# Projection products turned over: weight columns stationary, tokens moving, TensorE in program order

## The chip, the cores and the metric

The kernel runs on one core of one Trainium2 chip. The metric is the device time of one execution in microseconds (us). Five engines work side by side, each with a queue of its own that it takes in order: TensorE (PE in the profile; PEld is its weight load), VectorE (DVE), ScalarE (ACT), GpSimd (POOL) and SyncE (SP), which issues the transfers here.

## The reference

One layer of an encoder: 256 tokens, 2048 channels, all in float32. A bidirectional gated recurrence (16 heads of 128 keys and 128 values) and a gated feed-forward network with a width-3 convolution over tokens, each between RMS norms and with a residual.

```python
h = rmsnorm(x, norm_pre_mix)
u = h @ w_in                                   # 2048 -> [q | f_fwd | f_bwd | v | g], 2048 each
q = silu(q);  f = lb + (1 - lb) * sigmoid(f_raw);  k = 1 - f
# both directions: S_t = diag(f_t) S_{t-1} + k_t v_t^T,  o_t = S_t^T q_t
m = (rmsnorm(o, g_norm) * silu(g)) @ w_out
x = x + rmsnorm(m, norm_post_mix)
h = rmsnorm(x, norm_pre_ffn)
up = dwconv3(h @ ffn_w_in, w_conv)             # 2048 -> 11264, convolution over tokens
x = x + rmsnorm((silu(gate) * val) @ ffn_w_out, norm_post_ffn)
```

## The kernel before

Every dense product is cut into chunks of 512 output columns: 20 chunks of `w_in` (q, f, b, g, v for four groups of four heads), 4 of `w_o`, 22 of `w_up` and 4 of `w_dn`. A chunk runs over its input rows in parts of 256 rows (8 parts for 2048 rows, 22 in `w_dn`). For each part the weights come by DMA into `raw`; ScalarE rounds them to a high half `whi` (line 130), VectorE subtracts to get the low half `wlo` (line 131). `prep` does this up to `LOOK` = 3 parts ahead, in 4 buffers. The tokens are split the same way into `xh` and `xl`, and hi\*hi + hi\*lo + lo\*hi are added up in PSUM.

In `gemm` the tokens are stationary: for each 128 input rows and each of two token blocks, three products of 512 weight columns (lines 173, 176, 177). The result has tokens on the partitions. The recurrence and the convolution need channels on the partitions, so `two_tiles` (line 196) transposes q, f, b and the up-projection with eight 128x128 transposes a chunk.

The small work is cut into steps, which wait in two lists, `soon` and `later`; `gemm` takes one step after each part. `do_scores` queues the decayed scores of a group: `diag`, then seven levels of a binary tree over tokens (`level`), then `across`. A level is eight products of 128 columns (line 394), then VectorE work on keys `ks`, queries `qs`, block products `bp` and a masked copy into `Sd`, and a gather into `kc` on ScalarE. A level needs what the level ahead of it left. `do_o` multiplies scores with v, normalises and transposes back.

A scheduler orders the instructions of each engine. It keeps a few TensorE instructions in the order of the code (in the "head" and "tail" chunks); the others it may move. PSUM has 8 banks: `ps_g` (4) for the dense products, `ps_t` (2) for transposes, `ps_s` (2) for scores.

Of the kernel before, what the change touches and what calls it, by code (L numbers as in the profile page):

```python
# [13 lines left out]
U8 = mybir.dt.uint8  # L14
# [18 lines left out]
# the parts of the first projection, four heads at a time  # L33
# [3 lines left out]
# columns of the packed per-partition parameters  # L37
# [9 lines left out]
def encoder_layer(  # L47
# [34 lines left out]
    mk = const.tile([P, NLEV - 1, P], U8, name="mk")  # L82
# [51 lines left out]

    def flush():
        while soon or later:
            step()

    def gemm(xh, xl, order="plain", need=None, pre=None, mid=None):
# [16 lines left out]
        for s, m in seq:  # L156
# [13 lines left out]
            for j in range(2):  # L170
                k = 2 * s + j
                a, b = xh[:, k, m * P : (m + 1) * P], xl[:, k, m * P : (m + 1) * P]
                mm = nc.tensor.matmul(ps[m], a, hi[:, j, :], start=(k == 0), stop=False)  # L173
                if j == 0 and (order == "head" and s < 4 or order == "tail" and m == 1 and s >= nsub - 4):
                    tc.keep_in_program_order(mm)
                nc.tensor.matmul(ps[m], a, lo[:, j, :], start=False, stop=False)  # L176
                nc.tensor.matmul(ps[m], b, hi[:, j, :], start=False, stop=(k == 2 * nsub - 1))  # L177
# [5 lines left out]

    def rsqrt_mean(dst, ss, n):
        V.tensor_scalar(dst, ss, 1.0 / n, EPS, op0=ALU.mult, op1=ALU.add)
        G.tensor_tensor(dst, dst, mneg[:, : dst.shape[1]], op=ALU.pow)

    def two_tiles(dst_fn, srcs, after=None):
        """Four 128-column tiles of two token blocks, transposed, later on."""

        def one(i):
            tp = ps_t.tile([P, 2, T], F32, name="tp", tag="tp")
            for j in range(2):
                for m in range(2):
                    c0 = (2 * i + j) * P
                    nc.tensor.transpose(tp[:, j, m * P : (m + 1) * P], srcs[m][:, c0 : c0 + P], ident)  # L196
# [7 lines left out]
    xh = acts.tile([P, KT, T], F32R, name="xh", tag="ah")  # L204
    xl = acts.tile([P, KT, T], F32R, name="xl", tag="al")
# [4 lines left out]
    mkf = spool.tile([P, NLEV - 1, P], F32, name="mkf")  # L210
# [17 lines left out]
    def load_rest():  # L228
        nc.sync.dma_start(prm[:, C_CW:], par[:, C_CW:])
        nc.sync.dma_start(mkf, masks.rearrange("p (l t) -> p l t", t=P))  # L230
        V.tensor_copy(mk, mkf)

    # the tensor engine reaches its full clock after some microseconds of work
    warm = ps_t.tile([P, 2, T], F32, name="tp", tag="tp")
    for i in range(WARM):
        nc.tensor.transpose(warm[:, 0, :P], ident, ident)

    # lower bounds of the forget gates: softmax over the layers, cumulative
    # sum, minus the first layer's value
# [12 lines left out]
    def split_x(k2):  # L252
        tp = ps_t.tile([P, 2, T], F32, name="tp", tag="tp")
        for j in range(2):
            k = 2 * k2 + j
            for m in range(2):
                nc.tensor.transpose(tp[:, j, m * P : (m + 1) * P], xs[:, m, k * P : (k + 1) * P], ident)  # L257
        for j in range(2):
            k = 2 * k2 + j
            w1 = prm[:, C_PRE + k : C_PRE + k + 1]  # L260
            S.activation(xh[:, k, :], tp[:, j, :], AF.Copy, scale=w1)
        for j in range(2):
# [3 lines left out]
                xl[:, k, :], tp[:, j, :], w1, xh[:, k, :].bitcast(F32), op0=ALU.mult, op1=ALU.subtract  # L266
# [16 lines left out]
    nop = lambda: None  # L283
    split_x(0)
    split_x(1)
    ps0 = gemm(xh, xl, pre=lambda s: split_x(s + 2) if 2 * s + 4 < KT else None)
    soon.extend([lambda q=q: square_x(q) for q in range(4)] + [mean_x])
    ps1 = gemm(xh, xl)
# [3 lines left out]
    # ------------------------------------------------------- HGRN2, both ways  # L292
    opool = pool(hstack, "oacts", side="right")
    oh = opool.tile([P, KT, T], F32R, name="oh")
    ol = opool.tile([P, KT, T], F32R, name="ol")
# [11 lines left out]

    def do_q(g):
        ps = gemm(xh, xl) if g else ps0
        qn = [nat.tile([P, 512], F32, name="qn", tag="qn") for _ in range(2)]  # L310
        for m in range(2):
            silu_nat(ps, m, qn[m])
        qT = hp.tile([P, HG, T], F32, name="qT", tag="qT")
        two_tiles(lambda i, tp: S.copy(qT[:, 2 * i : 2 * i + 2, :], tp), qn)
        st["q", g] = qT

    def do_f(g, d):
        ps = gemm(xh, xl) if g or d else ps1
        sn = [nat.tile([P, 512], F32, name="qn", tag="qn") for _ in range(2)]
        for m in range(2):  # L320
            S.activation(sn[m], ps[m], AF.Sigmoid, scale=rs1[:, m : m + 1])
# [7 lines left out]
        def put(i, tp):  # L329
            for j in range(2):  # L330
                h = 2 * i + j
                c = d * NH + g * HG + h
                V.tensor_scalar(
                    f[:, h, :], tp[:, j, :], lb1[:, c : c + 1], lb[:, c : c + 1], op0=ALU.mult, op1=ALU.add
# [6 lines left out]
        two_tiles(put, sn, rest)  # L341
# [4 lines left out]
    def halves(t, m, c0=0, n=HG * T):  # L346
        """Of t[2, heads * tokens], the first of two in the left halves of blocks
        of 2m tokens and the second in the right halves: block, half, token."""
        return cut(t, c0, [[2 * m, n // (2 * m)], [HG * T + m, 2], [1, m]])

    def do_scores(g):
        """All decayed scores of four heads, S^T[s, t]: a pair (s, t) is met at
        the level of the binary tree over tokens where the two part, left and
        right in one block of 2m tokens, with the decay as a product up to the
        halves' boundary times one from there on. Forward, s lies left and t
        right; backward the other way round, so that both share a product.
        ks and qs hold the keys (forward, backward) and the queries (backward,
        forward) decayed to their block's boundary, bp the blocks' products."""
# [7 lines left out]
        def diag(i):  # L366
# [3 lines left out]
            sc = ps_s.tile([P, HG, P], F32, name="sc", tag="sc")  # L370
            for j in range(HG):
                h, b = (HG * i + j) // 2, (HG * i + j) % 2
                sl = slice(b * P, (b + 1) * P)
                nc.tensor.matmul(sc[:, j, :], kc[0][:, h, sl], q[:, h, sl], start=True, stop=True)  # L374
# [10 lines left out]
        def level(lev):  # L385
            m = 1 << lev
            scs = []
            for i in range(2):
                sc = ps_s.tile([P, HG, P], F32, name="sc", tag="sc")
                for j in range(HG):  # L390
# [3 lines left out]
                    nc.tensor.matmul(sc[:, j, :], kc[0][:, h, sl], r, start=True, stop=True)  # L394
# [20 lines left out]
        def across(d):  # L415
            sc = ps_s.tile([P, HG, P], F32, name="sc", tag="sc")
            s0, t0 = d * P, (1 - d) * P
            for h in range(HG):
                nc.tensor.matmul(  # L419
# [4 lines left out]
        later.extend([lambda: diag(0), lambda: diag(1)])  # L424
# [277 lines left out]
```

## Time and profile before

| what | value |
|---|---|
| median of 3 runs (lowest to highest) | 1385.48 us (1385.19 to 1386.78) |
| span of the profiled execution, first to last instruction | 1383.9 us |
| time of the profiled execution beside its span | not listed apart from the span |
| mean granted TensorE clock | 0.998 |
| TensorE busy; weight load busy | 1372.2 us; 1148.5 us |
| VectorE busy; ScalarE busy | 862.4 us; 684.1 us |

The profile is of one execution. Its span stands 1.6 us under the median of the runs. Durations of matmuls overlap: one of 512 columns is shown 0.39 us long while the next starts 0.23 us after it, so the spacing of starts, not the duration, is what one product costs TensorE.

### The profile page before, as it was taken

Reading aid. Unit: us, or ns where it says so; the run is one execution under the profiler, and the core shown is the slowest. Engines: PE = TensorE matmul, PEld = TensorE weight load, DVE = VectorE, ACT = ScalarE, POOL = GpSimd, SP = SyncE. Lnnn points to the kernel's source line nnn. Section 1 sums busy time; section 2 is a strip of 40 time slices with the busy share of each in tenths; the row PEclk is TensorE's granted clock in tenths of the full one; section 3 lists DMA queues with packets and bytes.
Section 4 is the critical chain, followed back from the end, with each engine's and each line's share of the span. In section 5 each row is a group of like instructions: output and inputs, shape, how many; then the busy total and the mean of one; then the engine's idle time right before and its main releaser. Section 6 shows DMA issues by size and latency. Waiting matters only on the chain.

```text
span 1383.9 us, 16448 instructions
## 1 busy us (share of the span) xinstructions
PE 1372.2 (99%) x6562; PEld 1148.5 (83%) x6562; DVE 862.4 (62%) x1007; ACT 684.1 (49%) x899; POOL 13.5 (1%) x21
## 2 busy tenths in 40 slices
PE   8999999999999999999999999999999999999997
PEld 7888888888888888888888888888888888888886
DVE  6577657855785776567566565656566656444444
ACT  6644544444444445456555555555555554434342
POOL 0000000000000000000000000000000000000000
PEclk9999999999999999999999999999999999999999
DMA  8553454445444534663555555555555556555552
GB/s 315 183 188 125 149 174 164 149 140 182 165 152 153 174 130 159 242 255 105 188 197 181 194 182 183 183 182 183 185 184 186 184 192 225 186 199 193 185 205 97
DMA packets 36988, 249.08 MB, mean 180 GB/s; under 512 B 4144, under 2 KB 4784, under 8 KB 7472
## 3 DMA queue, kind: packets, MB, share of 16 engines
q1 hardware_dynamic: 36912, 248.04, 51.9%
q8 instruction: 51, 0.84, 0.2%
q14 instruction: 25, 0.20, 0.0%
HBM read 245.93 MB, written 2.10 MB: 179 GB/s over the span
## 4 chain that ended last, share of the span: by engine, by line
PE 98%; DMA 1%; issue 0%; SPq 0%; DVE 0%; ACT 0%; DVEq 0%; POOLq 0%; POOL 0%
PE pg L176 30%; PE pg L177 30%; PE pg L173 30%; PE sc L394 4%; PE tp L196 2%; DMA xs<-in_x 1%; PE sc L451 1%; PE sc L419 1%; PE sc L374 1%; PE sc L450 1%; PE tp L545 0%; PE tp L257 0%; DVE fw L639 0%; SPq L116 0%; SPq L213 0%
## 5 line engine op out<-in xcount | busy, mean ns | idle before, releaser
L131 DVE TENSOR_TENSOR wlo<-raw,whi 128x1024 fp32r<-128x1024 f32 (+1 forms) x457 | 557.2, 1221 | 426.1 <-ACT whi L130 425.7
L130 ACT CAST whi<-raw 128x1024 fp32r<-128x1024 f32 (+1 forms) x457 | 479.6, 1051 | 506.8 <-PE pg L177 486.9
L177 PE MATMUL pg<-whi,h2l 128*128 128x512 f32 x704 | 276.3, 392 | 0.0
L176 PE MATMUL pg<-wlo,h2h 128*128 128x512 f32 x704 | 276.2, 392 | 0.0
L173 PE MATMUL pg<-whi,h2h 128*128 128x512 f32 x704 | 276.1, 393 | 0.0
L173 PE MATMUL pg<-whi,xh 128*128 128x512 f32 x640 | 251.6, 395 | 0.0
L177 PE MATMUL pg<-whi,xl 128*128 128x512 f32 x640 | 251.4, 393 | 0.0
L176 PE MATMUL pg<-wlo,xh 128*128 128x512 f32 x640 | 250.9, 392 | 0.0
L177 PEld LDWEIGHTS pg<-whi,h2l 128*128 128x128 f32 x704 | 132.3, 188 | 28.3
L176 PEld LDWEIGHTS pg<-wlo,h2h 128*128 128x128 f32 x704 | 132.3, 188 | 26.2
L173 PEld LDWEIGHTS pg<-whi,h2h 128*128 128x128 f32 x704 | 132.2, 188 | 25.9
L177 PEld LDWEIGHTS pg<-whi,xl 128*128 128x128 f32 x640 | 120.2, 188 | 24.6
L176 PEld LDWEIGHTS pg<-wlo,xh 128*128 128x128 f32 x640 | 120.3, 188 | 23.4 <-DVE wlo L131 0.2
L173 PEld LDWEIGHTS pg<-whi,xh 128*128 128x128 f32 x640 | 120.3, 188 | 23.3
L177 PE MATMUL pg<-whi,gl 128*128 128x512 f32 x352 | 137.0, 389 | 0.0
L173 PE MATMUL pg<-whi,gh 128*128 128x512 f32 x352 | 137.0, 389 | 0.0
L176 PE MATMUL pg<-wlo,gh 128*128 128x512 f32 x352 | 137.0, 389 | 0.0
L176 PEld LDWEIGHTS pg<-wlo,gh 128*128 128x128 f32 x352 | 66.1, 188 | 13.8
L173 PEld LDWEIGHTS pg<-whi,gh 128*128 128x128 f32 x352 | 66.1, 188 | 13.7
L177 PEld LDWEIGHTS pg<-whi,gl 128*128 128x128 f32 x352 | 66.1, 188 | 13.6
L394 PEld LDWEIGHTS sc<-qs,kc 128*128 128x128 f32 x448 | 57.9, 192 | 2.2
L607 DVE SCALAR_TENSOR_TENSOR acc<-tp,prm,acc 128x255 f32<-128x255 f32 x88 | 41.8, 476 | 27.3 <-PE tp L196 27.3
(108 smaller groups left out, 1010.6 us busy)
## 6 DMA issues: line engine op xcount, KB each, us to landing
raw<-in_w_up SPq DMA_DIRECT2D x88, 1024.0 KB, 4.9
raw<-in_w_in SPq DMA_DIRECT2D x78, 1024.0 KB, 4.9
raw<-in_w_dn SPq DMA_DIRECT2D x44, 1024.0 KB, 4.9
raw<-in_w_o SPq DMA_DIRECT2D x16, 1024.0 KB, 4.9
x<-in_x SPq DMA_DIRECT2D x1, 2048.0 KB, 7.6
wp<-in_post SPq DMA_DIRECT2D x2, 1024.0 KB, 5.9
out<-fw SPq DMA_DIRECT2D x8, 256.0 KB, 2.5
xs<-in_x SPq DMA_DIRECT2D x3, 512.0 KB, 10.2
```

The lines of the kernel that those rows point to most:

```text
L130: S.copy(hi[:, j], src[:, j])
L131: V.tensor_tensor(lo[:, j], src[:, j], hi[:, j].bitcast(F32), op=ALU.subtract)
L173: mm = nc.tensor.matmul(ps[m], a, hi[:, j, :], start=(k == 0), stop=False)
L176: nc.tensor.matmul(ps[m], a, lo[:, j, :], start=False, stop=False)
L177: nc.tensor.matmul(ps[m], b, hi[:, j, :], start=False, stop=(k == 2 * nsub - 1))
L196: nc.tensor.transpose(tp[:, j, m * P : (m + 1) * P], srcs[m][:, c0 : c0 + P], ident)
L374: nc.tensor.matmul(sc[:, j, :], kc[0][:, h, sl], q[:, h, sl], start=True, stop=True)
L394: nc.tensor.matmul(sc[:, j, :], kc[0][:, h, sl], r, start=True, stop=True)
L419: nc.tensor.matmul(sc[:, h, :], ks[:, d, h, s0 : s0 + P], qs[:, 1 - d, h, t0 : t0 + P], start=True, stop=True)
L450: nc.tensor.matmul(o[:, h, :], Sd[:, 2 * h + b, :], v[:, b, cs], start=True, stop=False)
L451: nc.tensor.matmul(o[:, h, :], So[1 - b][:, h, :], v[:, 1 - b, cs], start=False, stop=True)
L607: V.scalar_tensor_tensor(a[:, 1:T], z[:, 0 : T - 1], cw[0], a[:, 1:T], op0=ALU.mult, op1=ALU.add)
```

## The change

The chunks of q, f, b (12 chunks) and of `w_up` but the first (21 chunks) go through a new function, `gemm_t`. There the weight columns are stationary and the tokens move: `xh` and `xl` lie side by side in one tile `xx` of 2 x 256 columns, so that one product of 512 columns with `whi` gives hi\*hi in the left half of a PSUM bank and hi\*lo in the right half, and a second product of 256 columns adds `wlo` times `xh` to the left half. Channels come out on the partitions, and the transposes of these chunks go. `each_token` adds the halves (a copy on ScalarE, an add on VectorE per 128 channels) and multiplies by the norm's factor per token, which `spread` lays out over the partitions with two small products. A chunk takes 4 PSUM banks instead of 2, so `ps_g` has 6, and scores share `ps_t` with the transposes. All TensorE instructions go through `mm` and `tr`, which keep them in the order of the code. The lists get empty steps (`nop`): a level every second step, `do_o` behind the scores in `later`. The masks come as bytes by DMA, behind the start-up loads.

```diff
+    def mm(out, a, b, **kw):
+        return tc.keep_in_program_order(nc.tensor.matmul(out, a, b, **kw))
+    def tr(out, a):
+        return tc.keep_in_program_order(nc.tensor.transpose(out, a, ident))
-    ps_g = pool(ctx, "ps_g", 4, space=bass.MemoryType.PSUM)
+    ps_g = pool(ctx, "ps_g", 6, space=bass.MemoryType.PSUM)
     ps_t = pool(ctx, "ps_t", 2, space=bass.MemoryType.PSUM)
-    ps_s = pool(ctx, "ps_s", 2, space=bass.MemoryType.PSUM)
...
+    def gemm_t(xx, need=None, pre=None):
+        ps = [ps_g.tile([P, 2, T], F32, name="pg", tag="pg") for _ in range(4)]
+        for s in range(nsub):
+            if pre:
+                pre(s)
+            prep(base + s + (LOOK if ci else 1))
+            hi, lo = parts[ci, s]
+            for n in range(4):
+                cs = slice(n * P, (n + 1) * P)
+                for j in range(2):
+                    k = 2 * s + j
+                    mm(ps[n], hi[:, j, cs], xx[:, k], start=(k == 0), stop=False)
+                    last = k == 2 * nsub - 1
+                    mm(ps[n][:, 0, :], lo[:, j, cs], xx[:, k, 0, :], start=False, stop=last)
+            step()
...
+    def spread(rs, name):
+        tp = ps_t.tile([P, 2, T], F32, name="tp", tag="tp")
+        for m in range(2):
+            a = rs[:, m : m + 1].broadcast_to([P, P])
+            mm(tp[:, 0, m * P : (m + 1) * P], a, ident, start=True, stop=True)
+        S.copy(name, tp[:, 0, :])
...
+    def each_token(ps, dst, r):
+        for i, p in enumerate(ps):
+            z = dst[:, i, :]
+            S.copy(z, p[:, 1, :])
+            V.tensor_tensor(z, p[:, 0, :], z, op=ALU.add)
+        V.tensor_tensor(dst, dst, r[:, None, :].broadcast_to([P, len(ps), T]), op=ALU.mult)
...
     def do_q(g):
-        ps = gemm(xh, xl) if g else ps0
...
-        two_tiles(lambda i, tp: S.copy(qT[:, 2 * i : 2 * i + 2, :], tp), qn)
+        ps = gemm_t(xx) if g else ps0
+        each_token(ps, qT, r1)
+        S.activation(sg, qT, AF.Sigmoid)
+        V.tensor_tensor(qT, qT, sg, op=ALU.mult)
...
-        later.extend([lambda: diag(0), lambda: diag(1)])
-        later.extend([lambda lev=lev: level(lev) for lev in range(NLEV)])
-        later.extend([lambda: across(0), lambda: across(1)])
+        later.extend([nop, lambda: (diag(0), diag(1))])
+        for lev in range(NLEV):
+            later.extend([nop, lambda lev=lev: level(lev)])
+        later.extend([nop, lambda: (across(0), across(1))])
...
-        soon.extend([lambda: one(0), lambda: one(1)])
-        two_tiles(put, og)
+        queue = soon if g == NG - 2 else later
+        queue.extend([nop, lambda: one(0), lambda: one(1), nop])
+        two_tiles(put, og, queue)
...
     def up(c, done):
-        ps = gemm(h2h, h2l) if c else ps0
+        ps = gemm_t(hh) if c else ps0
...
+        z = [fn.tile([P, 2, T], F32, name="un", tag="un") for _ in range(2)]
+        for i in range(2):
+            each_token(ps[2 * i : 2 * i + 2], z[i], r2)
+        soon.extend([lambda: put(0, z[0]), lambda: put(1, z[1]), lambda: done(acc)])
```

Three places show how instructions move. The first is TensorE at the start, from the warm-up transposes (`tp<-ident`) on. Transposes `tp<-ident,xs` turn x; eight of them are one 512 KB piece of x. Before:

```order
L236 MATMUL tp<-ident 128x128 x18
L257 MATMUL tp<-ident,xs 128x128 x8
L173 MATMUL pg<-whi,xh 128x512
L176 MATMUL pg<-wlo,xh 128x512
L173 MATMUL pg<-whi,xh 128x512
L176 MATMUL pg<-wlo,xh 128x512
L177 MATMUL pg<-whi,xl 128x512
```

Now:

```order
L140 MATMUL tp<-ident 128x128 x18
L140 MATMUL tp<-ident,xs 128x128 x12
L137 MATMUL pg<-xx,whi 128x512
L137 MATMUL pg<-xx,wlo 128x256
L137 MATMUL pg<-xx,whi 128x512
L137 MATMUL pg<-xx,wlo 128x256
```

Four more transposes, which read the third piece of x, stand ahead of the first dense product; and the products come as pairs of 512 and 256 columns.

The second place is ScalarE around the end of the second chunk (f of group 0) and the start of the third (b). `qT` are the queries, `pg` the PSUM tiles of a chunk. Before:

```order
L130 CAST whi_449<-raw_447 128x1024
L303 ACT_TABLE_LOAD
L303 ACTIVATE sg_536<-pg_161,rs1_142 128x512
L303 ACTIVATE sg_539<-pg_162,rs1_142 128x512
L130 CAST whi_469<-raw_447 128x1024
```

Now (`pg_380` to `pg_383` are the four tiles of the f chunk):

```order
L224 COPY rt_79<-tp_562 128x256
L129 CAST whi_657<-raw_631 128x1024
L356 ACT_TABLE_LOAD
L356 ACTIVATE qn_610<-qT_600 128x1024
L347 COPY qn_613<-pg_380 128x256
L347 COPY qn_613<-pg_381 128x256
L347 COPY qn_613<-pg_382 128x256
L347 COPY qn_613<-pg_383 128x256
```

The table load stood in the middle of the second chunk and read two PSUM tiles of the first; now it and a sigmoid of 1024 columns stand ahead of the four copies that empty the f chunk's PSUM tiles.

The third place is VectorE between the b chunk of a group and its diagonal scores, which read `kc`. Before:

```order
L131 TENSOR_TENSOR wlo_778<-raw_775,whi_777 128x1024
L333 TENSOR_SCALAR f_559<-tp_743,lb1_132,lb_131 128x256 x2
L333 TENSOR_SCALAR f_559<-tp_766,lb1_132,lb_131 128x256 x2
L131 TENSOR_TENSOR wlo_802<-raw_775,whi_801 128x1024
L338 TENSOR_SCALAR ks_560<-f_559 128x1024
L339 TENSOR_TENSOR qs_561<-qT_542,f_559 128x1024
L405 TENSOR_TENSOR bp_857<-f_559 128x1024
L369 TENSOR_TENSOR kc_793<-ks_560 128x1024
```

Now:

```order
L130 TENSOR_TENSOR wlo_844<-raw_821,whi_843 128x1024
L348 TENSOR_TENSOR qn_805<-pg_630,qn_805 128x256
L349 TENSOR_TENSOR qn_805<-qn_805,rt_79 128x1024
L130 TENSOR_TENSOR wlo_864<-raw_861,whi_863 128x1024
L375 TENSOR_SCALAR f_624<-qn_805,lb1_127,lb_126 128x256 x4
L130 TENSOR_TENSOR wlo_880<-raw_861,whi_879 128x1024
L380 TENSOR_SCALAR ks_625<-f_624 128x1024
L381 TENSOR_TENSOR qs_626<-qT_600,f_624 128x1024
L447 TENSOR_TENSOR bp_959<-f_624 128x1024
L411 TENSOR_TENSOR kc_895<-ks_625 128x1024
```

The row of work up to `kc` stays, with the adds and the multiplication of `each_token` ahead of it; on TensorE the diagonal scores that wait for `kc` now stand at a fixed place, behind the fourth part of the chunk after b; the scheduler had put those of group 0 behind the sixth.

More of the change, by code (lines that the diff above doesn't have):

```diff
@@ L171, in gemm @@
                 k = 2 * s + j
[L172 to L177, printed above, removed]
+                a, b = (xx[:, k, i, m * P : (m + 1) * P] for i in range(2))
+                mm(ps[m], a, hi[:, j, :], start=(k == 0), stop=False)
+                mm(ps[m], a, lo[:, j, :], start=False, stop=False)
+                mm(ps[m], b, hi[:, j, :], start=False, stop=(k == 2 * nsub - 1))
             if m == 1 or order == "head" and s < 4:
@@ L182, in gemm @@
         return ps
+    def gemm_t(xx, need=None, pre=None):
+        ci = at["chunk"]
+        at["chunk"] += 1
+        nsub = 2 * chunks[ci][2]
+        base = subs.index((ci, 0))
+        ps = [ps_g.tile([P, 2, T], F32, name="pg", tag="pg") for _ in range(4)]
+        for s in range(nsub):
+            if s == need:
+                flush()
+            if pre:
[10 more added lines that the diff above has]
+            step()
+        return ps
     def rsqrt_mean(dst, ss, n):
@@ L195, in one @@
                     c0 = (2 * i + j) * P
-                    nc.tensor.transpose(tp[:, j, m * P : (m + 1) * P], srcs[m][:, c0 : c0 + P], ident)
+                    tr(tp[:, j, m * P : (m + 1) * P], srcs[m][:, c0 : c0 + P])
             dst_fn(i, tp)
@@ L199, in one @@
                 after()
-        soon.extend([lambda: one(0), lambda: one(1)])
-    xh = acts.tile([P, KT, T], F32R, name="xh", tag="ah")
-    xl = acts.tile([P, KT, T], F32R, name="xl", tag="al")
+        queue.extend([lambda: one(0), lambda: one(1)])
+    xx = acts.tile([P, KT, 2, T], F32R, name="xx", tag="xx")
     hstack = ExitStack()
@@ L229, in load_rest @@
         nc.sync.dma_start(prm[:, C_CW:], par[:, C_CW:])
-        nc.sync.dma_start(mkf, masks.rearrange("p (l t) -> p l t", t=P))
-        V.tensor_copy(mk, mkf)
     warm = ps_t.tile([P, 2, T], F32, name="tp", tag="tp")
     for i in range(WARM):
-        nc.tensor.transpose(warm[:, 0, :P], ident, ident)
+        tr(warm[:, 0, :P], ident)
     lbr = prm[:, C_LB : C_LB + 2 * NH].rearrange("p (n l) -> p n l", l=1)
@@ L256, in split_x @@
             for m in range(2):
-                nc.tensor.transpose(tp[:, j, m * P : (m + 1) * P], xs[:, m, k * P : (k + 1) * P], ident)
+                tr(tp[:, j, m * P : (m + 1) * P], xs[:, m, k * P : (k + 1) * P])
         for j in range(2):
@@ L293, in encoder_layer @@
     opool = pool(hstack, "oacts", side="right")
[L294 to L295 removed]
+    oo = opool.tile([P, KT, 2, T], F32R, name="oo")
+    mk = opool.tile([P, NLEV - 1, P], U8, name="mk")
+    nc.sync.dma_start(mk, masks.rearrange("p (l t) -> p l t", t=P))
     rstack = ExitStack()
@@ L544, in split @@
             for j in range(4):
-                nc.tensor.transpose(tp[:, j, :], x2[:, m, n * 512 + j * P : n * 512 + (j + 1) * P], ident)
+                tr(tp[:, j, :], x2[:, m, n * 512 + j * P : n * 512 + (j + 1) * P])
             for j in range(4):
@@ L578, in encoder_layer @@
     rsqrt_mean(rs2, sx2, D)
+    r2 = const.tile([P, T], F32, name="rt", tag="rt")
+    spread(rs2, r2)
     bstack.close()
```

110 lines of the change are left out of this document (54 added, 56 removed).

## The prediction

> **What bounds the kernel now.** I read the page's busy times and its chain of waits first, then the waits by engine, then stretches of one stage each.
>
> ```profile
> PE 1372.2 (99%) x6562; PEld 1148.5 (83%) x6562; DVE 862.4 (62%) x1007; ACT 684.1 (49%) x899; POOL 13.5 (1%) x21
> PE 98%; DMA 1%; issue 0%; SPq 0%; DVE 0%; ACT 0%; DVEq 0%; POOLq 0%; POOL 0%
> ...
> PE tp L257 <- DMA xs<-in_x: 2.4, 2, 1.8
> PE tp L236 <- POOL ident masks.py:199: 1.4, 1, 1.4
> ```
>
> TensorE is on the chain for 98% of the span, and in the whole run it waits twice for x (2.4 us) and once for the identity (1.4 us). It is a queue that never runs dry, so the time is the sum of the spacings of its products. Work taken from it counts in full; every wait that appears on it counts in full too. The spacings come from two stretches, `w_o` chunk 3 with nothing but 96 products of 512 columns, and twenty chunks of the up-projection:
>
> ```profile
> 589.06:610.82 21.76, 21.76 (x97) 18.02 (x96) 12.18 (x12) 11.49 (x14) 0.00 (x0) 1.00 0.54 192
> 658.13:1112.71 454.58, 454.58 (x2082) 375.23 (x2080) 283.20 (x340) 245.21 (x302) 0.35 (x1) 1.00 0.54 186
> ```
>
> The first gives 21.76 / 96 = 226.7 ns for a wide product (512 columns). The second gives 454.58 / 20 = 22.73 us a chunk; it has eight transposes beside the 96 products, so a transpose costs (22.73 - 21.76) / 8 = 0.121 us with the disturbance around it.
>
> **What is removed.** The twelve q, f, b chunks and 21 of the 22 up chunks lose eight transposes each: 264 x 0.121 = **-32.0 us**, all on the path. What ScalarE and VectorE did with them goes too, and is off the path.
>
> **What replaces it.** Per 128 rows and chunk, six wide products (1360 ns) become four pairs of a wide and a narrow one (256 columns). The moved columns are the same, 3072; the products go from 6 to 8. So everything hangs on the narrow one's spacing: each ns over 113.4 (half of 226.7) costs 33 x 64 = 2112 times that, 2.1 us. No row shows this shape. The nearest:
>
> ```profile
> 709.45 0.60 PE L196 MATMUL tp<-ident,un 128*128 128x128 f32 x4
> 363.15 1.95 PE L374 MATMUL sc<-qT,kc 128*128 128x128 f32 x16
> L374 PE MATMUL sc<-qT,kc 128*128 128x128 f32 x64 | 7.8, 275 | 0.0
> L374 PEld LDWEIGHTS sc<-qT,kc 128*128 128x128 f32 x64 | 7.8, 191 | 0.3
> L173 PEld LDWEIGHTS pg<-whi,h2h 128*128 128x128 f32 x704 | 132.2, 188 | 25.9
> ```
>
> A row of 16 score products is 1.95 us long, the last 0.275: spacing (1.95 - 0.275) / 15 = 111.7 ns, each with its own weight load. For transposes, (0.60 - 0.27) / 3 = 110 ns. The loads of scores are shown 191 ns long, those of dense products 188; since score products follow each other every 111.7 ns, a load of this kind does not hold TensorE for 188. So the low end is 109 (transposes, rounded down), the high end 226.7 (the width saves nothing). I take 115: half of the wide one, and 1.6 ns for a part that doesn't shrink; it lies by the rows of 110 and 112, the fastest at which weights are changed here. Then a pair is 341.7 against 340.0 ns: **+3.6 us** (-9 at 109, +14 at 120, +236 at 226.7). `spread` adds four small products, **+0.5**.
>
> [...]
>
> **What the fixed order costs.** Where the scheduler let TensorE go round a wait, it now stands. I followed the new order of each queue with durations of before; VectorE instructions that follow each other without waiting overlap by about 0.08 us.
>
> *Start.* The first dense product now stands behind the transposes of the third piece of x.
>
> ```profile
> 1.36 4.10 PE L236 MATMUL tp<-ident 128*128 128x128 f32 x18 [1.36 <-POOL ident masks.py:199]
> 7.93 0.63 PE L257 MATMUL tp<-ident,xs 128*128 128x128 f32 x4 [1.81 <-DMA xs<-in_x]
> 8.32 0.48 PE L173 MATMUL pg<-whi,xh 128*128 128x512 f32 x1
> ...
> 12.31 1.06 PE L257 MATMUL tp<-ident,xs 128*128 128x128 f32 x8 [0.55 <-DMA xs<-in_x]
> ```
>
> That piece lands at 12.3. Before, dense products began at 8.32; now at 12.31 + 4 x 0.11 = 12.75. The chunk then takes 21.9 us and 20 more transposes (2.4), ending at 37.0 instead of 33.76: **+3.3**. And TensorE idles from 8.4 to 12.3, with only four transposes since 6.1. What that does to the clock:
>
> ```profile
> 5.80:9.21 3.41, 1.60 (x11) 1.26 (x10) 2.03 (x4) 1.97 (x5) 0.00 (x0) 1.00 1.01 308
> 1374.55:1377.96 3.41, 1.39 (x7) 0.81 (x5) 1.52 (x4) 0.69 (x2) 0.54 (x1) 1.00 0.61 218
> 1377.96:1383.90 5.94, 0.00 (x0) 0.00 (x0) 2.34 (x4) 0.00 (x0) 0.00 (x0) 0.50 0.49 177
> ```
>
> The granted clock (third from the end) is 1.00 behind a stretch of 3.41 us with 1.60 of work, 0.50 behind one with 1.39. The warm-up row shows the low clock's price: (4.10 - 0.4) / 17 = 0.22 us a transpose, twice the 0.11. After 12.3 I expect half speed for about 3.2 us: **+1.6** (0.7 to 2.5).
>
> *First b chunk.* ScalarE loads a table, runs a sigmoid and only then empties the f chunk's PSUM tiles.
>
> ```profile
> L303 ACT ACT_TABLE_LOAD x1 | 1.3, 1283 | 0.0
> L130 ACT CAST whi<-raw 128x1024 fp32r<-128x1024 f32 x455 | 478.3, 1053 | 503.7 <-PE pg L177 486.9 <-DVE ks L338 8.5 <-DMA raw<-in_w_in 3.0
> L616 ACT ACTIVATE acc<-acc 128x1024 f32<-128x1024 f32 x11 | 11.6, 1057 | 0.0
> L602 ACT ACTIVATE acc<-tp,prm 128x256 f32<-128x256 f32 x88 | 37.1, 477 | 35.4 <-PE tp L196 35.4
> L339 DVE TENSOR_TENSOR qs<-qT,f 128x1024 f32<-128x1024 f32 x8 | 9.7, 1218 | 0.0
> ```
>
> From the f chunk's end: a cast whose buffer comes free then (1.05), the load (1.28), the sigmoid (1.06), while VectorE still has q's multiplication (1.22) ahead of its adds: first tile free at about 3.45 + 1.22 + 0.48 (an add of that size taken as long as the copy) = 5.15 us. Four of six banks are the f chunk's, so b's third tile needs it after two tiles of work, 1.37 us: **+3.8**. A gap that long takes the work of one or two stretches of 3.41 under 1.4 us: half speed again, **+1.0**. [...] In the other chunks the first tile is free about when the chunk ends, 1.4 us early.
>
> *Diagonal scores*, at their fixed place after four parts (10.9 us after the b chunk):
>
> ```profile
> 354.50 0.69 DVE L338 TENSOR_SCALAR ks<-f 128x1024 f32<-128x1024 f32 x1
> 355.11 1.22 DVE L339 TENSOR_TENSOR qs<-qT,f 128x1024 f32<-128x1024 f32 x1
> 356.24 1.22 DVE L405 TENSOR_TENSOR bp<-f 128x1024 f32<-128x1024 f32 x1
> 357.38 1.22 DVE L369 TENSOR_TENSOR kc<-ks 128x1024 f32<-128x1024 f32 x1
> ```
>
> These four take 4.1 us, ending 12.7 us after that b chunk (345.89). In the new order they follow the fourth `wlo` of the next chunk, which can't end before 7.8: `kc` at 11.9, four groups x 1.0 = **+4.0** (0 to 7).
>
> *Levels.* In two steps TensorE works 2 x 2.72 + 8 x 0.112 = 6.3 us; VectorE, by the rows below, two `wlo`, `ks`, `qs` and two masked copies, 2 x 1.22 + 1.21 + 1.22 + 2 x 0.74 less six overlaps = 5.9. I cost them at nothing; the cover is 0.4 us a level.
>
> ```profile
> L413 DVE COPY_PREDICATED Sd<-mk,sc 128x512 f32<-128x512 uint8 x48 | 35.3, 735 | 12.3 <-PE sc L394 12.2
> L398 DVE TENSOR_TENSOR ks<-ks,bp 128x1024 f32<-128x1024 f32 x24 | 29.0, 1209 | 0.0
> L131 DVE TENSOR_TENSOR wlo<-raw,whi 128x1024 fp32r<-128x1024 f32 x455 | 555.9, 1223 | 423.6 <-ACT whi L130 423.2
> ```
>
> *Ends.* The last group's transposes are flushed inside the first `w_o` chunk, and the norm factor goes through TensorE behind the first up chunk, where ScalarE waited for it:
>
> ```profile
> L186 POOL TENSOR_TENSOR ro<-ro,mneg 128x4 f32<-128x4 f32 x8 | 8.1, 1010 | 503.4 <-DVE ro L185 503.4
> L468 ACT ACTIVATE oh<-tp,prm 128x512 fp32r<-128x512 f32 x8 | 5.1, 685 | 6.2 <-PE tp L196 6.2
> 658.51 1.27 ACT L594 ACTIVATE un<-pg,rs 128x512 f32<-128x512 f32 x2 [1.85 <-POOL rs L186]
> ```
>
> Squares (1.0), factor (0.2 + 1.0) and four products (1.1) stand between the last scores and the flush, against one part of 2.7: 0.8 us, and 0.7 for the split (0.685): **+1.5**. The factor came 0.4 us after the chunk's end at 658.13: **+0.5**.
>
> *Queues.* SyncE's bytes of masks now wait for x's last reader with weights queued behind, some 5 us before those weights must be issued: nothing. GpSimd keeps its work. VectorE gains at most 33 x (4 x 0.48 + 1.22) = 104 us and ScalarE 33 x 4 x 0.48 = 63 from `each_token`: 70% and 54% busy.
>
> **Sum.** -32.0 + 3.6 + 0.5 + 3.3 + 1.6 + 3.8 + 1.0 + 4.0 + 1.5 + 0.5 = -12.2: a span of 1371.7, and with the 1.6 us by which the runs' median stands above this profile's span, **1373 us**.
>
> **Rivals.**
> - *No waits* (the fixed order costs nothing, so it and the wider steps do nothing): -32.0 + 4.1 = 1358. For it: before, TensorE never waited for VectorE. Against: x cannot land earlier. Chance 0.08.
> - *Narrow product at the floor*, 109: 1361 with my waits. For it: two rows of 110 to 112 with half the columns. Chance 0.12. [...]
> - *Waits at every chunk's edge*: `each_token` comes late by 0.3 us of its 1.4 us cover at 33 edges, +10: 1383 (1380 to 1390). For it: VectorE's 104 us more, all at the edges. Against: the order puts the adds first. Chance 0.20.
> - *Slower: the narrow product doesn't cover the weight load.* It decides from 115 + 12.2 / 2.112 = 120.8 ns; at the load's shown 188 it would be 1373 + 154 = 1527. Against: scores at 111.7 with loads of 191. Chance 0.08.
>
> The forecast itself (1366 to 1380) has 0.52. About 0.2% is what a measurement here can tell from no change: 1382.7 to 1388.3. Range 1360 to 1386: below lie parts of the first two rivals, above part of the third and the slower one. Faster 0.78 (forecast, two rivals, a third of the third), same 0.11, slower 0.11.
>
> **What would show it.** An up chunk of 21.9 us (22.73 now); the first product at 12.7; granted clock 0.5 behind it; one wait of some 4 us in the first b chunk for VectorE; four of 1 us for `kc`. Wrong, if up chunks take over 22.5 us, or waits for VectorE on TensorE pass 20 us in sum.

## The result: 12 us slower, and the profile after

The changed kernel took 1398.14 us (median of 4 runs, 1397.63 to 1399.16), the kernel before 1386.13 in the same comparison (1385.19 to 1386.83): ratio 1.0088, 95% interval 1.0074 to 1.0102. Forecast were 1373 us, 1360 to 1386. The profiled run spans 1396.8 us, 12.9 more than before. Its page and its chain of waits:

```profile
span 1396.8 us, 18404 instructions
...
PE 1373.8 (98%) x7362; PEld 1180.3 (84%) x7362; DVE 935.1 (67%) x1188; ACT 698.7 (50%) x971; POOL 12.4 (1%) x21
...
PE 96%; DVE 2%; ACT 1%; issue 1%; DMA 0%; SPq 0%; DVEq 0%; POOLq 0%; POOL 0%; ACTq 0%
```

TensorE still carries the end. What it waits for (us in total, times, longest):

```profile
PE sc L137 <- DVE kc L411: 4.1, 4, 1.0
PE pg L137 <- DVE qn L348: 3.7, 1, 3.7
PE tp L140 <- DVE wlo L130: 3.4, 1, 3.4
PE tp L140 <- DMA xs<-in_x: 1.4, 1, 1.4
PE tp L140 <- POOL ident masks.py:199: 1.4, 1, 1.4
PE pg L137 <- DVE oo L512: 0.6, 1, 0.6
PE tp L140 <- DVE og L504: 0.2, 1, 0.2
```

That is 14.8 us against 3.8 before, and the large ones had been forecast. What had not been is the pace of the products. `w_o` chunk 2 and nineteen up chunks (2 to 20), and the groups of the second stretch:

```profile
603.82:625.58 21.76, 21.76 (x98) 18.02 (x97) 11.91 (x11) 11.30 (x14) 0.00 (x0) 1.00 0.56 196
696.81:1126.46 429.65, 429.65 (x2434) 372.52 (x2433) 315.01 (x439) 235.00 (x323) 0.00 (x0) 1.00 0.54 186
...
L137 PE MATMUL pg<-hh,whi 128*128 128x512 f32 x1217 | 430.1, 399 | 0.0
L137 PE MATMUL pg<-hh,wlo 128*128 128x256 f32 x1217 | 341.8, 281 | 0.0
```

The old form in `w_o` is as it was, 21.76 us a chunk. An up chunk takes 429.65 / 19 = 22.61 us; 22.73 before, 21.9 forecast. It holds nothing but 64 pairs of a wide and a narrow product, so a pair costs 429.65 / 1216 = 353.3 ns, where 341.7 was forecast and 340 is what six wide products made of it before. Starts of products one by one:

```profile
799.27 0.40 PE L137 MATMUL pg<-hh,whi 128*128 128x512 f32 x1
799.51 0.28 PE L137 MATMUL pg<-hh,wlo 128*128 128x256 f32 x1
799.63 0.40 PE L137 MATMUL pg<-hh,whi 128*128 128x512 f32 x1
799.87 0.28 PE L137 MATMUL pg<-hh,wlo 128*128 128x256 f32 x1
799.98 0.40 PE L137 MATMUL pg<-hh,whi 128*128 128x512 f32 x1
800.22 0.28 PE L137 MATMUL pg<-hh,wlo 128*128 128x256 f32 x1
800.33 0.40 PE L137 MATMUL pg<-hh,whi 128*128 128x512 f32 x1
...
800.69 0.40 PE L137 MATMUL pg<-hh,whi 128*128 128x512 f32 x1
```

From wide to wide: 0.36, 0.35, 0.35, 0.36. In the trace's ns the pairs take 361, 349 and 350 in turn, with wide spacings of 241, 236 and 233 and narrow ones of 120, 113 and 117. So from the narrow product's start to the next one it takes about what was forecast, and the **wide one behind it became longer** than its 226.7. In the first projection some stretches between two groups of score products run in this rhythm of three, others at 346.7 a pair (343 and 350 in turn). Counting stretches of five pairs and more, 1724 pairs are in the first rhythm and 315 in the second, and none changes within a stretch.

### The profile page after: what moved, and what is told of

Same layout as the page of the kernel before. It is cut to its first block, busy times and chain, and to the rows that moved or that the text cites. A ratio compares the mean times of both kernels' runs of the same rounds, so it can differ in the third digit from the quotient of the medians.

```text
span 1396.8 us, 18404 instructions
## 1 busy us (share of the span) xinstructions
PE 1373.8 (98%) x7362; PEld 1180.3 (84%) x7362; DVE 935.1 (67%) x1188; ACT 698.7 (50%) x971; POOL 12.4 (1%) x21
## 4 chain that ended last, share of the span: by engine, by line
PE 96%; DVE 2%; ACT 1%; issue 1%; DMA 0%; SPq 0%; DVEq 0%; POOLq 0%; POOL 0%; ACTq 0%
PE pg L137 89%; PE sc L137 6%; PE tp L140 1%; ACT whi L129 1%; DVE wlo L130 1%; DMA raw<-in_w_in 0%; DVE bp L447 0%; DVE kc L411 0%; DVE ks L380 0%; DVE fw L692 0%; SPq L115 0%; ACT L356 0%; DVE qT L357 0%; ACT qn L356 0%; PE tp L137 0%
## 5 line engine op out<-in xcount | busy, mean ns | idle before, releaser
L137 PE MATMUL pg<-hh,whi 128*128 128x512 f32 x1344 | 475.2, 399 | 0.0
L137 PE MATMUL pg<-hh,wlo 128*128 128x256 f32 x1344 | 377.5, 281 | 0.0
L137 PEld LDWEIGHTS pg<-hh,whi 128*128 128x128 f32 x1344 | 252.5, 188 | 63.0
L137 PE MATMUL pg<-xx,whi 128*128 128x512 f32 x768 | 276.2, 403 | 3.7 <-DVE qn L348 3.7
L137 PEld LDWEIGHTS pg<-hh,wlo 128*128 128x128 f32 x1344 | 253.9, 189 | 0.0
L137 PE MATMUL pg<-whi,gg 128*128 128x512 f32 x704 | 217.0, 389 | 0.0
L137 PE MATMUL pg<-xx,wlo 128*128 128x256 f32 x768 | 216.4, 282 | 0.0
L137 PEld LDWEIGHTS pg<-xx,whi 128*128 128x128 f32 x768 | 145.9, 190 | 37.6 <-issue 4.0
L137 PE MATMUL pg<-whi,xx 128*128 128x512 f32 x512 | 165.2, 395 | 0.0
L137 PEld LDWEIGHTS pg<-xx,wlo 128*128 128x128 f32 x768 | 146.8, 191 | 0.0
```

The costliest lines, as they stand in the source:

```text
L137: return tc.keep_in_program_order(nc.tensor.matmul(out, a, b, **kw))
```

## The experiments

**Which property of the narrow product costs.** Nine forms of the pair, two up chunks each; up chunk c, from 1 to 18, runs form (c - 1) // 2:

```diff
-                    mm(ps[n], hi[:, j, cs], xx[:, k], start=(k == 0), stop=False)
...
-                    mm(ps[n][:, 0, :], lo[:, j, cs], xx[:, k, 0, :], start=False, stop=last)
+            products(ps, hi, lo, xx, s, 2 * nsub, way(ci))
```

> What a pair of products (a wide one of 512 columns, a narrow one of 256) costs when only its neighbours change. In the changed kernel a pair takes 353.4 ns in the up stage, and the sum had taken 341.7. Up chunks 1 to 18 run nine forms here, two chunks each: 0 as in the changed kernel; 1 in groups wide, wide, narrow, narrow; 2 eight wide, then eight narrow; 3 each narrow one behind the wide one of the next bank; 4 the wide one cut into two of 256 (three narrow); 5 the narrow one made 512 wide (adds a term that the reference does not have); 6 the narrow one of 128 columns (half of its term left out); 7 the narrow one with a weight of 64 columns (half of its term left out); 8 all cut to 128 columns (six). Theory A, each change of width costs 6.7 ns: forms 1 to 8 take 347, 341, 353, 340, 453, 297, 353, 340 ns a pair. Theory B, each product has a fixed part of about 27 ns besides 0.39 ns a column, whatever runs beside it: 353, 353, 353, 380, 453, 303, 353, 460. Theory C, the weight load of the next product needs about 127 ns and a narrow product hides only part of it: 353, 353, 353, 380, 453, 353 (a shorter product hides less), under 353 (a shorter load), 760. Theory D, a narrow product waits for the wide one that wrote the same bank: form 3 about 341, the others as form 0.

The run took 1448.13 us (one run). Measured, ns a pair in the second chunk of each form (form 2: the first, since the second has a wait for VectorE): 353.3 (form 0), 348.3 (1), 349.2 (2), 352.5 (3), 360.0 (4), 453.3 (5), 341.0 (6), 346.8 (7), 670 (8), and in up chunk 20, again form 0, **346.7**. Groups of form 4, of form 5 and of form 8, each in the window of its two chunks:

```profile
L137 PE MATMUL pg<-hh,whi 128*128 128x256 f32 x256 | 46.1, 283 | 0.0
L137 PE MATMUL pg<-hh,wlo 128*128 128x256 f32 x130 | 36.7, 283 | 0.0
...
L137 PE MATMUL pg<-hh,whi 128*128 128x512 f32 x129 | 50.2, 389 | 0.0
L137 PE MATMUL pg<-hh,wlo 128*128 128x512 f32 x128 | 49.9, 390 | 0.0
...
L137 PE MATMUL pg<-hh,whi 128*128 128x128 f32 x512 | 78.0, 275 | 0.0
L137 PE MATMUL pg<-hh,wlo 128*128 128x128 f32 x256 | 49.5, 275 | 0.0
```

384 products of 256 columns in 46.08 us are 120.0 each; 256 of 512 in 58.06 us are 226.8; 768 of 128 in 85.7 us are 111.6. From 512 to 256 columns the spacing falls by 106.7, which is 0.417 ns a column, and 13.3 stay in both: **a fixed part**, so that a pair costs 226.7 + 120.0 = 346.7 by the two uniform streams, which is also the best that such pairs ran at in turn. At 128 columns it no longer falls by that line: 53.3 + 13.3 would be 66.7, and 111.6 was measured. What holds it there is not shown.

Theory A falls (form 4 would be 340), C with its 127 ns a load too (form 4 would be 380, form 8 760), D too (form 3). B's kind is right, its size not: 13.3 and not 27. But the same form 0 ran at 353.3 in chunk 2 and at 346.7 in chunk 20, so the other 6.7 belong to no operand and no size. Form 8 has a load for each product and 111.6 ns from one to the next, so a load need not hold TensorE for longer than that, and a narrow product at 117 is longer. Form 7 decides less than it seems: it shortens the narrow product's own load (138 ns on the record instead of 188), but the wide one's load, which starts with the narrow product (62.74 us for both in the changed kernel), keeps its 188. It ran at 346.8, no better than form 0 at its best; whether the wide one's load has a part in the other 6.7 is not shown. How a pair splits between its two starts says little: in form 6 the narrow product of 128 columns takes 60 ns to the next start and the wide one 280.

**Which part of the change costs.** The up stage alone in the old form:

```diff
-        ps = gemm_t(hh) if c else ps0
+        ps = gemm(hh) if c else ps0
...
-        if c == 0:
+        if True:
```

> The changed kernel with the up stage alone put back to the form of before (tokens stationary, 96 products of 512 columns a chunk, then eight transposes). If the trace's account is right, the up stage gained only 0.12 us a chunk, 2.4 us in all, and lost 1.2 us at its first chunks: 1398 + 1 = about 1399 us, within 0.2% of the changed kernel. If the pairs of the up stage are what made the kernel slower, it falls to about 1386. If the form of the up stage gains what the prediction said (0.84 us a chunk), it rises to about 1415.

1399.78 us (1399.49 to 1400.14), ratio 1.0095 (1.0078 to 1.0112): as the trace's account has it. Its up chunks take 22.71 us, 22.61 in the new form: 21 chunks of new products save 2 us, not 18.

All products in the old form, so that TensorE's fixed order, the wider steps, the banks and the mask transfer are left:

```diff
-        ps = gemm_t(xx) if g else ps0
+        ps = gemm(xx) if g else ps0
...
-        each_token(ps, qT, r1)
...
+        two_tiles(lambda i, tp: S.copy(qT[:, 2 * i : 2 * i + 2, :], tp), qn, soon)
```

> The changed kernel with all products back in the form of before (tokens stationary, transposes), so that the instructions of TensorE in the program's order, the scores at every second step, the six and two banks and the other mask transfer are all that is left of the change. Theory, by the trace's account: the start (5.7 us by the end of the first f chunk) and the waits for kc (4) are the order's and stay, the up stage is as before; the wait of the first b chunk is each_token's and goes: about 1386.7 + 10 = 1397 us (1394 to 1400). Rival, the order costs nothing and the new products with their adding of halves cost it all: 1387. Rival, the transposes, now in the program's order, wait for the sigmoids at every edge of q, f and b: above 1402.

1397.24 us (1396.17 to 1398.01), ratio 1.0077 (1.0061 to 1.0092). What is left of the change costs 11 us by itself, and the new products with their adding of halves come out even. The order, the steps, the banks and the mask transfer are not told apart here. Its waits, where those for `kc` and the one at the start remain and the one in the first b chunk is gone:

```profile
PE sc L136 <- DVE kc L410: 3.3, 4, 0.8
PE tp L139 <- DVE wlo L129: 3.2, 1, 3.2
PE tp L139 <- DMA xs<-in_x: 1.9, 1, 1.9
```

**Fewer changes of width.** Two wide, then two narrow products, in all 33 chunks:

```diff
                     mm(ps[n], hi[:, j, cs], xx[:, k], start=(k == 0), stop=False)
+                for j in range(2):
+                    k = 2 * s + j
...
                     mm(ps[n][:, 0, :], lo[:, j, cs], xx[:, k, 0, :], start=False, stop=last)
```

> The changed kernel with the products of a part and column tile in the order wide, wide, narrow, narrow, in all 33 chunks of the new form. Theory A (each change of width costs 6.7 ns): 2112 x 6.7 = 14 us less, about 1384 us. Theories B and C (fixed part, or the load): 1398 us, unchanged. Theory D (same bank): unchanged or a few us more.

1389.04 us (1388.00 to 1390.15), ratio 1.0016 (1.0007 to 1.0025). None had this: two thirds of theory A's gain. Every undisturbed stretch now has 348.3 a pair, whatever comes before it; this order shows one rhythm only in this run.

Eight wide, then eight narrow:

> The changed kernel with all eight wide products of a part ahead of its eight narrow ones, in all 33 chunks of the new form. Theory A: 2112 x 11.7 = 25 us less, about 1374 us, below the kernel before. Theories B and C: 1398 us. A narrow product needs only the low part of the weights, which VectorE makes last, so at the start and where the first product waits for VectorE up to 1 us may fall away in any theory.

1422.53 us (1422.31 to 1422.78), ratio 1.0258 (1.0243 to 1.0274): slower, and not by the pairs (349.2 where nothing waits):

```profile
PE pg L137 <- DVE un L352: 17.0, 20, 0.9
PE pg L137 <- DVE qn L352: 5.8, 4, 3.2
...
PE pg L137 <- DVE qT L352: 4.1, 3, 1.5
```

A chunk's third bank is now needed after four wide products, 0.9 us, instead of four pairs, 1.4; and the first bank of the chunk before is finished six narrow products before that chunk's end, 0.7 us, instead of six pairs, 2.1. With 1.9 us less room the adds of `each_token` come late, by up to 0.9 us in the up stage; with those for q, f and b the waits are 27 us in sum, where the changed kernel had 3.7. The prediction's third rival, waits at every chunk's edge, is what happens here; by that the changed kernel had about 1 us to spare (1.9 less 0.9, an estimate).

**What chooses the rhythm.** Breaks in the middle of up chunks:

```diff
+            kind = c % 4 if s == 4 and c > 1 else 0
+            if kind in (1, 3):
+                dm = ps_t.tile([P, 2, T], F32, name="dm", tag="tp")
+                for i in range(kind):
+                    tr(dm[:, 0, :P], ident)
...
+                if kind == 2 and n == 0:
+                    todo = [(0, 0), (1, 0), (0, 1), (1, 1)]
```

> In the changed kernel 1327 pairs of the up stage follow one another without a break and every third of them takes 361 ns instead of 347 (349, 350, 361: 353.3 in the mean), while undisturbed stretches of the same pairs in the first projection ran at 346.7. Here the stream of the up stage is broken in the middle of up chunks 2 and later: by one transpose nobody reads (chunks 5, 9, 13, 17, 21), by three (3, 7, 11, 15, 19), by a changed order of one group, wide wide narrow narrow (2, 6, 10, 14, 18); chunks 4, 8, 12, 16, 20 have no break. Theory E, two rhythms: the pairs settle at each break on 346.7 or on 353.3 and keep that until the next break; both are found behind the 15 breaks, and a chunk without one goes on as the chunk before it ended. Rival F, the place: in the up stage (its tiles, its transfers) a pair always takes 353.3; every stretch is at 353.3. Rival G, chance: the rhythm changes without a break too. Time: 1398 + 15 x 0.2 for the transposes, less 0.43 us for each chunk at 346.7, so 1393 to 1401.

1395.67 us (one run). Behind the five single transposes the pairs ran at 353.3, behind the five changed groups at 346.7, behind the three transposes three times at 346.7 and twice at 353.3. No stretch changed without a break, chunks without one among them. Theory E stands; F and G fall.

One changed group in every part, on the kernel with fewer waits (below):

```diff
+                if n == 0:
+                    todo = [(0, 0), (1, 0), (0, 1), (1, 1)]
```

> The kernel with fewer waits (1376.7), with only the first of the four groups of a part in the order wide, wide, narrow, narrow and the other three in the order wide, narrow, wide, narrow. In the run with breaks, all five stretches that began with one such group ran at 346.7 ns a pair, and the order wide, wide, narrow, narrow throughout gave 348.4. Theory E, the rhythm is chosen at the group that starts a stretch: 2112 x (348.4 - 347) = 2 to 3 us less, about 1374 us, with no stretch at 353.3. Rival: those five were all at the same place of a chunk, and elsewhere such a group can also leave the pairs at 353.3: between 1374 and 1385, with up chunks of 22.6 us instead of 22.29. Rival: what sets the rhythm is how often the order changes, so that three swapless groups a part are too few to lock: up chunks between 22.2 and 22.3, 1376.

1379.15 us (1377.74 to 1379.97), ratio 0.9946 (0.9932 to 0.9959): 2.4 more than without, where 2 to 3 less were expected. Three parts of eight pairs, one after the other:

```profile
771.75:774.57 2.82, 2.82 (x19) 2.46 (x17) 2.82 (x6) 2.13 (x4) 0.00 (x0) 1.00 0.36 145
774.57:777.34 2.77, 2.77 (x18) 2.42 (x17) 2.77 (x6) 1.96 (x3) 0.00 (x0) 1.00 0.73 243
777.34:780.16 2.82, 2.82 (x18) 2.45 (x17) 2.82 (x6) 1.05 (x1) 0.00 (x0) 1.00 0.32 134
```

The two rhythms take turns, so the first rival was right: such a group can also leave the pairs in the slow one. I took it for a switch that turns the rhythm over, and tried it once, in the first group of up chunk 2 of the changed kernel:

```diff
+                if (ci - C_UP, s, n) == (2, 0, 0):
+                    todo = [(0, 0), (1, 0), (0, 1), (1, 1)]
```

> The changed kernel with one single group of four products in another order: the first of up chunk 2 goes wide, wide, narrow, narrow; all else, instructions and operands, as it was. In the run before, each such group turned the rhythm over: parts of 2777 ns (347.1 a pair) and of 2817 ns (352.1) took turns. The changed kernel enters the up stage at 353.3. Theory E, the group turns it over and nothing turns it back: 20 chunks x 64 pairs x 6.7 ns = 8.5 us less, about 1389.6 us, with up chunks of 22.19 us from the second on. Rival, the rhythm falls back by itself or the group has an effect on its neighbours alone: 1398, up chunks of 22.61.

1398.53 us (1397.76 to 1399.24), ratio 1.0082 (1.0066 to 1.0099): wrong, the 1278 pairs behind it stay at 353.3. The group had begun at the wide product of 236 ns, those that had worked at 241 and at 232 or 233. So the same two and four pairs later, with `(2, 0, 1)` and `(2, 0, 2)`:

> As the kernel before (one group in another order, up chunk 2), with the second group of the part in its place, two pairs later. There the group began with a wide product that took 236 ns, the middle one of the slow rhythm's three (241, 236, 233), and the pairs stayed at 353.3. In the run with breaks the groups behind which the pairs ran at 346.7 began at 241 and at 232. Theory H, where in the cycle of three the group falls decides: two pairs later it begins at 241, and all pairs behind it run at 346.7: 20 x 64 x 6.7 ns = 8.5 us less, about 1389.8 us. Rival, one group early in the stage cannot do it: 1398, up chunks of 22.61.

> The same with the third group of the part, four pairs later, which begins at 233, the last of the three. Theory H: the pairs behind it run at 346.7, about 1389.8 us. If only one place of three does it: 1398.

1388.81 us (median of 9; ratio 1.0027, 1.0011 to 1.0044) and 1390.08 (one run). In the first, 18 up chunks behind the group:

```profile
718.97:1118.33 399.36, 399.36 (x2306) 349.14 (x2305) 295.46 (x415) 222.61 (x306) 0.00 (x0) 1.00 0.54 190
```

399.36 / 1152 = 346.7 a pair, 22.19 us a chunk. Four products in another order, of 7362, take 9 us away, and the same change two pairs earlier took nothing away: same instructions, operands, banks and transfers otherwise. Eight of the nine executions lie between 1388.3 and 1390.7, one took 1398.5, the time without the swap; it has no trace here, and may have come in at another place of the cycle. What inside TensorE makes the two rhythms stays open.

**Taking the waits away.** On the order wide, wide, narrow, narrow:

```diff
-            if pre:
-                pre(s)
             prep(base + s + (LOOK if ci else 1))
...
+            if pre:
+                pre(s)
             step()
...
-        each_token(ps, qT, r1)
...
+        add_halves(ps, qT)
...
+        soon.append(rest)
...
-            V.tensor_tensor(qq, st["q", g], f, op=ALU.mult)
+            if d:
+                st["kc", g] = hp.tile([P, HG, T], F32, name="kc", tag="kc")
+                tc.keep_in_program_order(V.tensor_tensor(st["kc", g], st["k", g][:, 0], kk, op=ALU.add))
+            tc.keep_in_program_order(V.tensor_tensor(qq, st["q", g], f, op=ALU.mult))
```

Here `rest` is the multiplication by `r1`, the sigmoid and its product, which now stand behind the next chunk's copies. (39.46 and 33.76 in the text below are the ends of the first q chunk alone.)

> The changed kernel with four edits. The order wide, wide, narrow, narrow, which alone gave 1389.0. Splits of x behind the products of a part instead of ahead of them, so that the first product no longer stands behind transposes that wait for x's third load: q0 and f0 ended at 39.46 us, and 33.76 in the kernel before. The first q chunk's sigmoid behind the copies of the first f chunk, which takes away the wait of 3.7 us in the first b chunk and the half clock behind it (1.6). kc ahead of qs on VectorE, where four groups waited 1.0 us each. Theory: the waits add up, 1389.0 - 5 - 5 - 4 = 1375 us (1373 to 1379). Rival: at the start the transfers of x and of the weights set the pace, so that nothing but the sum of the later waits falls away, 1380. Rival: the waits only move to the next buffer, 1386 to 1389.

1376.71 us (1376.57 to 1377.53), ratio 0.9931 (0.9919 to 0.9944): **below both kernels**. Its waits:

```profile
PE tp L140 <- DMA xs<-in_x: 2.3, 1, 2.3
PE tp L140 <- POOL ident masks.py:199: 1.4, 1, 1.4
PE pg L137 <- DVE oo L523: 0.6, 1, 0.6
PE pg L137 <- DVE xx L301: 0.5, 1, 0.5
PE tp L140 <- DVE og L515: 0.2, 1, 0.2
```

The theory of adding waits holds: 12.3 us less than the same order with them, for 14 forecast. The first product comes at 9.76 (12.89), the first b chunk takes 22.29 us (28.04).

## Why the prediction was wrong, point by point

**The step that failed is "What replaces it", the pair at 341.7 ns, +3.6 us.** Measured: 1724 x 13.3 + 315 x 6.7 = +25.0 us over 340, and up chunks of 22.61, past the 22.5 that had been named as the sign of being wrong. Two errors are in it. First, the narrow product was priced at half of the wide one and 1.6 ns "for a part that doesn't shrink", because score products and transposes lay at 110 to 112. Those rows are the floor of 128-column products (111.6 here), not the slope; the fixed part is 13.3, in the wide product's 226.7 already, so it doesn't halve with the columns. The pair is then 346.7: 6.7 ns more, 14 us over 2112 pairs, the forecast's own "120" end. Second, the wide product was left at 226.7 with a narrow one ahead of it, for which no row stood: in the rhythm of three a pair costs another 6.7. The records put nearly all of the excess on the wide product (232 in the fast rhythm, 236.5 in the slow one) and leave the narrow one at 115 and 117, where the forecast had it. So the 115 was met and the pair was still too dear: the pair, not the share of either product, is what is shown. The ends of the term, 109 to 226.7, moved the narrow product alone. (The far end is misadded: 226.7 makes +239.5 over 340, not +236.) The last rival, a weight load that isn't covered, had put the turning point at 120.8 ns for the narrow one. That was measured at 117 and yet the kernel became slower, since the point should have been set for the pair (347.5, and 353.3 came). Its mechanism is not shown: a load costs no more than 111.6 where each product has one, and what makes the second 6.7 stays open.

**Transposes removed, -32.0:** held. In the kernel with the old products in the new order an up chunk is 22.71 us, 0.95 over the 21.76 of pure products; the forecast had 0.97. The new pairs gave 0.85 of that back, per chunk 64 x 13.3 ns.

**Start, +3.3 and +1.6:** held in size; the first chunk ends at 39.46, 5.7 later, for 4.9 forecast. First product at 12.89, forecast 12.75, behind the transposes of x's third piece. (The view names VectorE's `wlo` as the one waited for; in the first run with one swap, whose start is the same, it names the transfer of x.)

```profile
12.16 1.08 PE L140 MATMUL tp<-ident,xs 128*128 128x128 f32 x4 [3.35 <-DVE wlo L130]
...
12.89 0.77 PE L137 MATMUL pg<-xx,whi 128*128 128x512 f32 x1
...
13.68 0.63 PE L137 MATMUL pg<-xx,whi 128*128 128x512 f32 x1
14.11 0.41 PE L137 MATMUL pg<-xx,wlo 128*128 128x256 f32 x1
14.32 0.63 PE L137 MATMUL pg<-xx,whi 128*128 128x512 f32 x1
...
14.00:15.00 1.00, 1.00 (x5) 0.81 (x5) 0.85 (x2) 1.00 (x3) 0.00 (x0) 1.00 1.13 434
```

0.64 us from wide to wide is half speed, for six pairs: the pairs at a granted 0.50 in the first b chunk take the same. The 1.00 in the last row (third from the end) is no sign against it: this trace holds no record of the clock before 17.34 us, and the view prints 1.00 where there is none. The spacings change at just that time, from 427 and 213 ns to 236 and 123. What came ahead of it was not quite the forecast's account. Here the transposes at 5.3 and at 8.0 us already follow every 213 ns, so by the spacings the clock had not yet risen, where the forecast had it fall in the gap from 8.4 to 12.3. That the size fits is partly luck. In the first run with one swap the clock did rise early. By its records it fell at 7.80, ahead of the gap that the forecast named, and was low until 14.63. The stretch ahead of the fall, and the last low one:

```profile
4.39:7.80 3.41, 1.05 (x10) 0.81 (x8) 0.87 (x2) 0.91 (x2) 0.00 (x0) 1.00 0.75 244
11.22:14.63 3.41, 2.88 (x11) 2.62 (x12) 2.14 (x4) 1.82 (x5) 0.00 (x0) 0.50 1.04 406
```

**First b chunk, +3.8 and +1.0:** held, in the order forecast: table load, sigmoid, copies, q's product, adds.

```profile
63.29 1.28 ACT L356 ACT_TABLE_LOAD   x1
...
64.59 1.06 ACT L356 ACTIVATE qn<-qT 128x1024 f32<-128x1024 f32 x1
65.55 1.18 ACT L347 COPY qn<-pg 128x256 f32<-128x256 f32 x4
65.67 1.23 DVE L357 TENSOR_TENSOR qT<-qT,qn 128x1024 f32<-128x1024 f32 x1 [1.14 <-ACT qn L356]
66.82 1.41 DVE L348 TENSOR_TENSOR qn<-pg,qn 128x256 f32<-128x256 f32 x4
...
67.38 0.47 PE L137 MATMUL pg<-xx,whi 128*128 128x512 f32 x1 [3.66 <-DVE qn L348]
...
69.00:70.00 1.00, 1.00 (x5) 0.90 (x4) 0.48 (x1) 0.81 (x1) 0.00 (x0) 0.50 0.06 16
```

A wait of 3.7, then the clock at 0.50 from 68.5 to 71.9: five pairs at 0.64 us, 1.4 for the 1.0 forecast. It fell 1.2 us after the products had begun again, behind this stretch:

```profile
65.12:68.53 3.41, 1.15 (x7) 1.04 (x8) 2.82 (x6) 1.60 (x5) 0.00 (x0) 1.00 0.81 288
```

That is 1.15 us of work in 3.41 with 2.3 us of idling: the clock fell behind it, as it had behind 1.39 in the kernel before and, at 7.80 in the row above, behind 1.05. Behind 1.60, in the kernel before, it stayed at 1.00. The forecast's reading by work holds for these four stretches; that the work is what sets the clock is not shown.

**Diagonal scores, +4.0:** 4.1, four waits of 1.0. **Levels, 0:** no row of them among the waits. **Ends, +1.5 and +0.5:** the first `w_o` chunk grew by 2.0 (28.14 to 30.16), 0.5 more than forecast. The first up chunk grew by 0.35 (24.62 to 24.97), and that is the four products of `spread` themselves. **Waits at every edge** did not come in the changed kernel.

So the terms outside the pairs, -15.8 in sum, came out near -12: with +25.0 the sum is +12.7, the shift of the last product (1375.55 to 1388.27). Some 2 us of the difference of 3.5 I have not traced.

## What to carry to other kernels

Price a product of a new shape by a line through two widths of its own kind (here 226.7 ns at 512 columns and 120.0 at 256), as long as it lies above the floor of short products (111.6 at 128 columns here), and not by the nearest row of another kind; set the break-even on the repeating group, since a neighbour can pay (here the wide product, 236.5 for 226.7). Where products of different widths alternate, read their spacings one by one; an order with longer runs of equal width had a single rhythm here (two and two: 348.3 ns a pair), and is worth trying as long as the banks still come free in time (eight and eight: 27 us of waits). A fixed order makes everything wait that stands behind a late operand: it was worth 12 us to place three things (a split, a sigmoid, an addition) by when their operands arrive.

## What the hardware showed that I had not expected

- The same pairs run at 346.7 or 353.3 ns, steady over up to 1327 pairs; the choice falls where a stretch begins and out of the slow one depends on where in the cycle of three a changed group falls (begun at 236: slow again; at 241, 232 or 233: fast). Out of the fast one, in the run with a group in every part, the up chunks looked at always went to the slow one.
- Wide spacing of fp32r products was 226.7 in runs of equal width (`w_o`; 226.8 in form 5); two and two gave 233 for each wide one and 115 for each narrow one.
- At half speed the fixed part is gone: 427 and 213 ns for 512 and 256 columns, at a granted clock of 0.50 (68.5 to 71.9 us in the changed kernel).
- The granted clock has no record ahead of its first one, at 17.34 us in the changed kernel's trace; the view reads 1.00 there, at spacings about twice as long (427 and 213 ns, 236 and 123 from then on). At the start of a program the spacings are the safer sign.
